# Other start addresses for six small tiles: 128 bytes more in each, taken from the dynamic transfers' scratch

## The chip, the cores and the metric

The kernel runs on one core of one Trainium2 chip. The metric is the device time in microseconds of one execution; the median of three runs before the change is 1042.14 us (1041.03 to 1042.35).

## The reference

One layer of a bidirectional encoder on 512 tokens of width 1024, in float32:

```
x += 1/2 * g1 * SwiGLU_1(mod(RMSNorm(x)))                                  # FFN 1
x += g2 * W_out( sig(gA) * W_A(WindowGQA+sink) + sig(gB) * W_B(DiffAttn) ) # the mixers
x += 1/2 * g3 * SwiGLU_2(mod(RMSNorm(x)))                                  # FFN 2
```

Shift, scale and gate of each step (`sh, sc, g`, nine vectors of 1024) come from a conditioning vector `c` through `w_mod`. `WindowGQA` is attention in a band of 128 positions (8 query heads, 2 key heads of 64); `DiffAttn` is dense attention of 4 heads, in which one softmax is taken from another, `p0 - lam * p1`. The gates `gA`, `gB` are 2 x 1024 columns of the mixers' input projection.

## The kernel before, in words

Everything lies transposed: 128 channels on the partitions, the 512 tokens along the free dimension. A float32 product is done as three products of type float32r: each operand is split into a high part and a low part (`split_from`, L188: ACT copies the high part, DVE subtracts, both counted under L189), and `mm3` (L172, its three matmuls are L173 to L175) adds high by high, high by low and low by high in PSUM. In the FFNs, `two` (L440, matmuls L446 to L448) does the same on halves of 256 tokens, in a Strassen-Winograd scheme (`Unit`) whose sums of weights are made by transfers that add into SBUF from the GpSimd queue (POOL). The matmuls of the mixers' first projections are L1168 to L1170 (512 columns) and L1187 to L1189 (`project_pairs`, 256 columns). The first operand of a matmul is called stationary here (128 columns of 4 bytes, loaded by its own instruction, PEld), the second moving (256 or 512 columns of 4 bytes).

The order of the work is fixed when the program is built: in some stages by hand (`manual_schedule`), in the mixers by a planner (`Line`) with fixed costs and due times, in which start addresses play no part.

All tiles lie in one SBUF pool. Every kind of tile has a tag and a fixed number of buffers; the buffers of a tag lie one behind another, and the tags in the order in which they are first asked for. Byte 0 on belongs to the scratch of dynamic transfers (4096 bytes a partition); the last tile ended at 229344 of 229376 bytes. In the built program the tiles that matter here began at these addresses in a partition:

| tile | what it holds | start, mod 128 | mod 256 |
|---|---|---|---|
| `high`, `low` | split weights, 5 slots of 4096 bytes each | 64; 0 with `ASIDE` (64 bytes on); 32 with `TURN` (96 bytes on) | 64; 128; 160 |
| `b8` | 12 tiles of 8192 bytes: hidden values, keys, values, activations | 64 | 64 |
| `raw`, `f2` | loaded weights; temporaries | 64 | 192 |
| `u4` | 6 tiles of 4096 bytes, see below | 32 | 160 |

`u4` (L157) serves many ends: columns of `w_mod` while a gate vector is made (`mod_load`, L240); operands of the FFNs' sums (`h_sum`, L589, the tile `n1`; `act_begin`, L1762, its last two spaces), where it is the moving operand of L446 to L448; weights that a transfer adds to (`Unit.place`, L469); small tables; and three uses that the change touches:

- **First gates' weights.** `load_split(..., spare=True)` (L210) puts the split weights of the first three gates into six `u4` tiles. `first_gates` (L1123) uses them as the stationary operand of `mm3`, in the hand-ordered stage between FFN 1 and the mixers (`boundary`, L360): 3 gates x 8 steps x 3 matmuls x 2 halves of 256 tokens = 144 matmuls. Between them stand small matmuls of the normalisation, L331 (`sums`) and L320 (`spread`).
- **Turned probabilities of the dense attention.** `diff_turn` (L1362) transposes the probabilities and splits them into two `u4` tiles; `diff_out` (L1379) takes 256 columns of them as the moving operand against `vb_h`, `vb_l` (in `b8`): 4 heads x 2 x 4 x 3 = 96 matmuls.
- **Turned probabilities of the window attention.** `window_turn` (L1598) and `window_out` (L1616) do the same with one `u4` tile per turn: 20 turns x 2 key heads x 3 = 120 matmuls against `vz` (in `b8`).

Of the kernel before, what the change touches and what calls it, by code (L numbers as in the profile page):

```python
# [12 lines left out]
F32R = mybir.dt.float32r  # L13
# [5 lines left out]
P = 128  # L19
D = 1024  # L20
T = 512
NC = D // P
# [111 lines left out]
def layer(ctx: ExitStack, tc: tile.TileContext, a: dict):  # L134
    nc = tc.nc
# [5 lines left out]
    def name(tag):  # L141
        count[0] += 1
        return f"{tag}_{count[0]}"

    def sbuf(tag, shape, dt, bufs):
        return sb.tile(shape, dt, name=name(tag), tag=tag, bufs=bufs)
# [7 lines left out]
    def b8(dt=F32R):  # L154
        return sbuf("b8", [P, 4, T], dt, 12)

    def u4(dt=F32R):  # L157
        return sbuf("u4", [P, 2, T], dt, 6)

    def small(n):  # L160
        return sbuf("sm", [P, 8], F32, 24)[:, 0:n]
# [4 lines left out]
    def keep(shape, nm, dt=F32):  # L166
        return sb.tile(shape, dt, name=nm, tag=nm, bufs=1)
# [20 lines left out]
    def split_from(hi, lo, src):  # L188
        last = S.copy(hi, src), V.tensor_tensor(lo, src, f(hi), ALU.subtract)  # L189
        split[:] = [i.ins for i in last]  # L190
# [5 lines left out]
    def high_low(n=1024, aside=0, holder=None):  # L196
        while turn[0] % HILO in holders:
            turn[0] += 1
        i = turn[0] % HILO
        turn[0] += 1  # L200
        if holder:
            holders[i] = holder
        i = i * 1024 + min(i, 2) * GAP + aside
        return tuple(t[:, i : i + n] for t in parts)
# [5 lines left out]
    def load_split(src, n=1024, spare=False, aside=0):  # L210
        raw = sbuf("raw", [P, 1024], F32, RAW)
        if spare:
            hi, lo = (u4().rearrange("p a b -> p (a b)") for _ in range(2))
        else:
            hi, lo = high_low(aside=aside)
        nc.sync.dma_start(raw[:, 0:n], src)
        split_from(hi[:, 0:n], lo[:, 0:n], raw[:, 0:n])
        return hi, lo
# [16 lines left out]
    parts, modv = [], []  # L235
# [4 lines left out]
    def mod_load(v, c, w=None):  # L240
        if w is None:
            w = u4(F32).rearrange("p a b -> p (a b)")
        nc.sync.dma_start(w, a["w_mod"][v * NC + c])
        return w
# [109 lines left out]
    def new_h():  # L354
        t = [b8() for _ in range(4)]
        hh = [t[c // 4][:, c % 4, :] for c in range(NC)]
        hl = [t[2 + c // 4][:, c % 4, :] for c in range(NC)]
        return hh, hl
# [245 lines left out]

    cact = [sbuf("ka", [P, D], F32, 1)]
    hh, hl = new_h()
    modv += [keep([P, NC], f"mod{v}") for v in range(len(modv), 9)]
    nc.scalar.dma_start(ccol, a["c"])
    tc.keep_in_program_order(nc.scalar.dma_start(par, a["par"]))
    for c in range(NC):  # L610
# [2 lines left out]
    with tc.manual_schedule(engines=BOUND | {mybir.EngineType.SP, mybir.EngineType.Pool}):  # L613
# [23 lines left out]
        def first_loads(k):  # L637
            scale = mod_load(SC1, k)
            if k == 0:
                kept.append(keep([P, NT], "pos", I32))  # L640
            shift = mod_load(SH1, k) if k == 0 else None
            raw = sbuf("raw", [P, 1024], F32, RAW)
            nc.sync.dma_start(raw, a["w1s"][k])
            w1[k] = [scale, shift or mod_load(SH1, k), raw]
# [52 lines left out]
        for k in range(3):  # L697
            first_loads(k)
# [91 lines left out]
        for k in range(1, NC):  # L790
# [21 lines left out]
            for outs in groups:  # L812
                for w, h in ((wh, hh[k]), (wh, hl[k]), (wl, hh[k])):
                    first_products(k, outs, w, h, FULL[0], False, k == NC - 1 and w is wl)
        loaded1 = [load_split(a["w1i"][0, k]) for k in range(2)]

    rest = [(v, c) for v in (G1, SC2, SH2, G2, SC3, SH3, G3) for c in range(NC)]
# [140 lines left out]
    with tc.manual_schedule(engines={mybir.EngineType.SP, mybir.EngineType.Pool}):  # L958
# [4 lines left out]
        for q in range(4, 2 * PLAIN):  # L963

            w, sums_from = loaded1, split[1]
            if q < 5:
                with tc.issue_after(split[0]), tc.issue_after(split[1]):
                    loaded1 = [load_split(a["w1i"][1, k]) for k in range(2)]
            behind = split[1]
            out = pair_banks()  # L970
            for k in range(NC):
                wh, wl = w[k // 4]
                for i in range(2):
                    o = (k % 4) * 256 + i * P
                    mm3(out[i], wh[:, o : o + P], wl[:, o : o + P], hh[k], hl[k], k == 0, k == NC - 1)
            with tc.issue_after(sums_from):
                for t in ("n1",) if q == 4 else ("n2", "t3", "t4"):
                    h_sum(t)
            with tc.issue_after(behind):
                finish(q, out)  # L980
            if q == 4:
                units1[PLAIN].prepare("s1")
            side1(1.0)
# [131 lines left out]
    def gate_end(j, out):  # L1115
        t = f2()
        S.activation(t, out, AF.Tanh, scale=0.5)
        S.dma_start(gate_scr[j], t)

    gate_w = [load_split(a["w_gate"][j], spare=True) for j in range(3)]  # L1120
    gate_out = {}

# [119 lines left out]
    def turned(srcs, tag="tp"):  # L1242

        tp = bank(tag)
        for j, src in enumerate(srcs):
            PE.transpose(tp[:, j * P : (j + 1) * P], src, ident)
        line.now += len(srcs) * TR
        line.free[tag] = line.helped(0.6, 0.8)
        return tp[:, 0 : len(srcs) * P]

    def cut(src, n):
        return [src[:, j * P : (j + 1) * P] for j in range(n)]
# [109 lines left out]
    def diff_turn(h, b, p):  # L1362

        tp = turned(cut(p, NT))
        turns["b"] += 1
        g, i = h * NT // 2 + b // 2, b % 2
        if i == 0:
            pair = [u4().rearrange("p a b -> p (a b)") for _ in range(2)]
            pt_b[g] = [t.rearrange("p (k i q) -> p k i q", k=NT, i=2) for t in pair]
        hi, lo = pt_b[g]  # L1370
        with tc.high_priority():
            split_from(hi[:, :, i, :], lo[:, :, i, :], tp.rearrange("p (k q) -> p k q", k=NT))
        if i == 1:
            line.at(
                line.free["tp"] + SLACK, lambda: diff_out(h, g),
                ("op" if g % 2 == 0 else "", lambda: turns["o"] == g + h),
            )

    def diff_out(h, g):  # L1379
        if g % 2 == 0:  # L1380
            out_b[h] = bank("op")
        hi, lo = pt_b[g]
        he = slice(h * P, (h + 1) * P)
        o = out_b[h][:, (g % 2) * 2 * P : (g % 2 + 1) * 2 * P]
        for k in range(NT):
            kh, kl = (t[:, k, :, :].rearrange("p i q -> p (i q)") for t in (hi, lo))
            mm3(o, vb_h[:, k, he], vb_l[:, k, he], kh, kl, k == 0, k == NT - 1)
        line.now += 2 * MM3
        turns["o"] += 1
        if g % 2:  # L1390
            t = f2()
            with tc.high_priority():
                S.copy(t, out_b[h])
            line.free["op"] = line.now + 1.0
            line.at(line.free["op"] + SLACK, lambda: diff_norm(h, t), ("op",))
# [137 lines left out]
    def span(b):  # L1533
        first, last = max(b - 1, 0), min(b + 1, NT - 1)
        return first, last - first + 1
# [59 lines left out]
    def turn_tag(b, g, kc):  # L1595
        return "acc" if (g + kc) % 2 else "tp"

    def window_turn(b, g, kc, sc):  # L1598
        tag = turn_tag(b, g, kc)
        tp = turned([sc[q][:, kc * P : (kc + 1) * P] for q in (0, 2, 1, 3)], tag)  # L1600
        pt = u4()
        with tc.high_priority():
            split_from(pt[:, 0, :], pt[:, 1, :], tp)
        i = g * span(b)[1] + kc
        line.at(
            line.free[tag] + SLACK, lambda: window_out(b, g, kc, pt),
            ("op" if i == 0 else "", lambda: turns["w"] == (b, i)),
        )
        if kc + 1 == span(b)[1]:
            turns["a"] += 1  # L1610
        else:
            line.at(line.now, lambda: window_turn(b, g, kc + 1, sc), (turn_tag(b, g, kc + 1),))
# [3 lines left out]
    def window_out(b, g, kc, pt):  # L1616
        first, nk = span(b)
        if g == 0 and kc == 0:
            out_a[b] = bank("op")
        o_ps = out_a[b]  # L1620
        for kv in range(2):
            vh, vl = (v[:, first + kc, kv, :, :].rearrange("p w d -> p (w d)") for v in wa["v"])
            ph, pl = (pt[:, i, kv * 2 * P : (kv + 1) * 2 * P] for i in range(2))
            mm3(
                o_ps[:, g * 2 * P : (g + 1) * 2 * P], vh, vl, ph, pl,
                kv == 0 and kc == 0, kv == 1 and kc == nk - 1,
            )
        line.now += MM3
        if g == 1 and kc == nk - 1:
            bq = slice(b * P, (b + 1) * P)  # L1630
            oa_h, oa_l = wa["o"]
            with tc.high_priority():
                split_from(oa_h[:, :, bq], oa_l[:, :, bq], o_ps.rearrange("p (g q) -> p g q", g=4))
            line.free["op"] = line.helped(0.6, 0.8)
            done["a"] += 1
            turns["w"] = (b + 1, 0)
        else:
            turns["w"] = (b, g * nk + kc + 1)
# [244 lines left out]
    with tc.manual_schedule(engines=BOUND):  # L1883
# [6 lines left out]
        at = TO_FFN2  # L1890
# [187 lines left out]
```

## Time and profile before

| what | value |
|---|---|
| median of three runs | 1042.14 us (1041.03 to 1042.35) |
| time of the profiled execution | 1040.55 us |
| its span, first to last instruction | 1038.8 us |
| PE, DVE, ACT, POOL busy | 1031.9, 786.8, 577.5, 167.7 us |
| DMA | 220.92 MB, 213 GB/s on average |

The span covers 1038.8 of the profiled execution's 1040.55 us, so 1.8 us lie around it. That execution is 0.5 us under the lowest of the three runs. Busy times of PE overlap, since one matmul's record (0.28 us for 256 columns) reaches over the start of the next two. So the cost of one more matmul is read from the timeline, as the distance between the starts of matmuls that follow each other; it is called the pitch here.

### The profile page before, as it was taken

The page shows a single profiled execution, that of the slowest core. Times are in us where ns is not written, and L with a number is a line of the kernel's source. Part 1 is how long each engine was busy: PE and PEld are TensorE (multiplying, and loading weights), DVE is VectorE, ACT ScalarE, POOL GpSimd, SP SyncE. Part 2 cuts the span into 40 slices and gives each one's busy share as a digit, 9 for nine tenths or more (in the row PEclk, how much of TensorE's full clock was granted, in tenths as well). Part 3 has the DMA queues.
Part 4 walks back from the last instruction along what each step waited for, and adds up shares of the span by engine and source line. Part 5 has one row for each costly group of instructions (what it writes and reads, how often), then busy time and mean ns, then how long its engine had stood idle before and what let it go on. Part 6 is the DMA issues. An engine that isn't in the chain of part 4 may idle for free.

```text
span 1038.8 us, 18730 instructions
## 1 busy us (share of the span) xinstructions
PE 1031.9 (99%) x7342; PEld 951.0 (92%) x7342; DVE 786.8 (76%) x1436; ACT 577.5 (56%) x952; POOL 167.7 (16%) x191
## 2 busy tenths in 40 slices
PE   9999999999999999999999999999999999999998
PEld 6889899899998998899888888989999999999998
DVE  7896667567797679859772588976899777877867
ACT  6665335244455333667785855525867546655553
POOL 2101110111100100543323101001112112212210
PEclk9999999999999999999999999999999999999999
DMA  9977887967884369796637934974498998989974
GB/s 366 357 231 203 237 235 219 254 153 225 233 202 156 129 219 409 236 263 150 173 79 183 270 123 157 377 231 100 97 237 193 237 235 207 227 223 214 204 153 112
DMA packets 68793, 220.92 MB, mean 213 GB/s; under 512 B 8288, under 2 KB 10976, under 8 KB 68704
## 3 DMA queue, kind: packets, MB, share of 16 engines
q1 hardware_dynamic: 46224, 146.52, 38.5%
q0 software_dynamic: 19344, 68.70, 35.9%
q10 hardware_dynamic: 3136, 4.51, 1.2%
q8 instruction: 57, 0.93, 0.4%
q14 instruction: 32, 0.26, 0.1%
HBM read 209.46 MB, written 10.23 MB: 211 GB/s over the span
## 4 chain that ended last, share of the span: by engine, by line
PE 94%; ACT 3%; DVE 3%; issue 0%; POOL 0%; DVEq 0%; ACTq 0%; POOLq 0%
PE acc L446 7%; PE acc L447 7%; PE acc L448 7%; PE sc L447 6%; PE sc L448 6%; PE sc L446 6%; PE sc L173 5%; PE sc L174 5%; PE sc L175 5%; PE acc L173 4%; PE acc L175 4%; PE acc L174 4%; PE acc L1168 2%; PE acc L1170 2%; PE acc L1169 2%; PE acc L691 1%
## 5 line engine op out<-in xcount | busy, mean ns | idle before, releaser
L189 ACT CAST high<-raw 128x1024 fp32r<-128x1024 f32 (+2 forms) x160 | 155.9, 985 | 151.3 <-PE sc L174 44.0
L189 DVE TENSOR_TENSOR low<-raw,high 128x1024 fp32r<-128x1024 f32 (+2 forms) x160 | 181.3, 1141 | 42.0 <-ACT high L189 40.6
L446 PE MATMUL acc<-b,high 128*128 128x256 f32 x508 | 140.8, 277 | 0.0
L447 PE MATMUL acc<-b,high 128*128 128x256 f32 x508 | 140.6, 277 | 0.1
L448 PE MATMUL acc<-b,low 128*128 128x256 f32 x508 | 140.5, 277 | 0.0
L447 PE MATMUL sc<-b,high 128*128 128x256 f32 x500 | 138.2, 276 | 0.0
L446 PE MATMUL sc<-b,high 128*128 128x256 f32 x500 | 138.1, 276 | 0.0
L448 PE MATMUL sc<-b,low 128*128 128x256 f32 x500 | 138.1, 276 | 0.0
L189 ACT CAST high<-u 128x1024 fp32r<-128x1024 f32 (+1 forms) x73 | 75.4, 1036 | 50.9 <-PE sc L174 19.9
L189 DVE TENSOR_TENSOR low<-u,high 128x1024 fp32r<-128x1024 f32 (+1 forms) x73 | 87.6, 1201 | 20.8 <-ACT high L189 19.0
L173 PE MATMUL sc<-b,high 128*128 128x512 f32 (+1 forms) x272 | 97.5, 358 | 0.0
L174 PE MATMUL sc<-b,high 128*128 128x512 f32 (+1 forms) x272 | 97.2, 357 | 0.0
L175 PE MATMUL sc<-b,low 128*128 128x512 f32 (+1 forms) x272 | 97.1, 357 | 0.0
L447 PEld LDWEIGHTS acc<-b,high 128*128 128x128 f32 x508 | 95.5, 188 | 0.4 <-DVE b L1862 0.3
L446 PEld LDWEIGHTS acc<-b,high 128*128 128x128 f32 x508 | 95.4, 188 | 0.3 <-ACT f L523 0.2
L448 PEld LDWEIGHTS acc<-b,low 128*128 128x128 f32 x508 | 95.4, 188 | 0.0
L446 PEld LDWEIGHTS sc<-b,high 128*128 128x128 f32 x500 | 93.9, 188 | 0.0
L448 PEld LDWEIGHTS sc<-b,low 128*128 128x128 f32 x500 | 93.9, 188 | 0.0
L447 PEld LDWEIGHTS sc<-b,high 128*128 128x128 f32 x500 | 93.9, 188 | 0.0
L173 PE MATMUL acc<-b,high 128*128 128x512 f32 (+1 forms) x240 | 89.2, 371 | 0.2 <-DVE u L189 0.2
L175 PE MATMUL acc<-b,low 128*128 128x512 f32 (+1 forms) x240 | 86.8, 362 | 0.0
L174 PE MATMUL acc<-b,high 128*128 128x512 f32 (+1 forms) x240 | 86.6, 361 | 0.0
(398 smaller groups left out, 2714.1 us busy)
## 6 DMA issues: line engine op xcount, KB each, us to landing
u<-w_mod SPq DMA_DIRECT2D x40, 512.0 KB, 8.4
b<-w_mod SPq DMA_DIRECT2D x32, 512.0 KB, 5.5
raw<-w2i SPq DMA_DIRECT2D x31, 512.0 KB, 5.2
u<-w2i POOLq DMA_DIRECT2D x31, 512.0 KB, 6.7
raw<-w1u SPq DMA_DIRECT2D x24, 512.0 KB, 6.9
u<-w1u POOLq DMA_DIRECT2D x24, 512.0 KB, 7.3
raw<-w1o SPq DMA_DIRECT2D x24, 384.0 KB, 4.6
raw<-w_gate SPq DMA_DIRECT2D x16, 512.0 KB, 5.3
```

Source lines behind the costliest of these rows:

```text
L173: PE.matmul(out, wh, xh, start=first, stop=False)
L174: PE.matmul(out, wh, xl, start=False, stop=False)
L175: PE.matmul(out, wl, xh, start=False, stop=last)
L189: last = S.copy(hi, src), V.tensor_tensor(lo, src, f(hi), ALU.subtract)
L446: PE.matmul(out, wh[:, s], xh, start=first and j == 0, stop=False, skip_group_check=True)
L447: PE.matmul(out, wh[:, s], xl, start=False, stop=False, skip_group_check=True)
L448: PE.matmul(out, wl[:, s], xh, start=False, stop=last and j == 1, skip_group_check=True)
L691: PE.matmul(out1[i][:, r], w[:, i * P : (i + 1) * P], h[:, r], start=first and r.start == 0, stop=last and r.stop == T, skip_group_check=True,
L1168: PE.matmul(out[t][:, 0:n], hh[k][:, ht], wh[:, o : o + n], start=k == 0, stop=False)
L1169: PE.matmul(out[t][:, 0:n], hh[k][:, ht], wl[:, o : o + n], start=False, stop=False)
L1170: PE.matmul(out[t][:, 0:n], hl[k][:, ht], wh[:, o : o + n], start=False, stop=k == NC - 1)
```

## The change

Each `u4` tile grows from 4096 to 4224 bytes, and its users get a view that begins `at` elements of 4 bytes into it: 8 (32 bytes) unless they ask for another place; the first gates' weights and both kinds of turned probabilities ask for 0. The scratch of dynamic transfers shrinks from 4096 to 2048 bytes a partition. The small tile `mod8` (the last of the nine gate vectors) is set up after the `u4` tiles instead of ahead of them.

```diff
-    def u4(dt=F32R):
-        return sbuf("u4", [P, 2, T], dt, 6)
+    def u4(dt=F32R, at=8):
+        return sbuf("u4", [P, 2 * T + 32], dt, 6)[:, at : at + 2 * T].rearrange("p (a b) -> p a b", a=2)
...
         if spare:
-            hi, lo = (u4().rearrange("p a b -> p (a b)") for _ in range(2))
+            hi, lo = (u4(at=0).rearrange("p a b -> p (a b)") for _ in range(2))
...
-    modv += [keep([P, NC], f"mod{v}") for v in range(len(modv), 9)]
+    modv += [keep([P, NC], f"mod{v}") for v in range(len(modv), 8)]
...
             if k == 0:
+                modv.append(keep([P, NC], "mod8"))
                 kept.append(keep([P, NT], "pos", I32))
...
-            pair = [u4().rearrange("p a b -> p (a b)") for _ in range(2)]
+            pair = [u4(at=0).rearrange("p a b -> p (a b)") for _ in range(2)]
...
-        pt = u4()
+        pt = u4(at=0)
...
-    nc = bacc.Bacc("TRN2", target_bir_lowering=False, num_devices=1, dynamic_dma_scratch_size=4096)
+    nc = bacc.Bacc("TRN2", target_bir_lowering=False, num_devices=1, dynamic_dma_scratch_size=2048)
```

No instruction is added, dropped or moved: on each of the five engines the built program holds the same instructions in the same order as before, apart from line numbers, running numbers in names and addresses. The same user gets the same one of the six `u4` buffers. What differs is where tiles lie:

- The six `u4` buffers begin at 165504 + 4224 i: 0 mod 128, and by turns 128 and 0 mod 256. A view at 8 begins at 32 mod 128, as before, by turns at 160 (as before) and at 32 mod 256. A view at 0 begins at 0 mod 128.
- Of the 144 matmuls of the first gates, 64 now have a stationary operand that starts from 128 mod 256, and 80 one from 0. Of the 216 with turned probabilities, 92 have a moving operand from 128 and 124 one from 0 mod 256. Of the 480 matmuls in the FFNs whose moving operand lies in `u4` (mod 128 unchanged), 264 start from 32 instead of 160 mod 256.
- All tiles ahead of `u4` move down by 2048 bytes, `raw`, `f2` and the tiles behind them by 1280 bytes. Both are multiples of 256, so nothing else changes mod 256.

## Prediction

> **What bounds the kernel now.** I read the page first: busy times, granted clock and the chain of work that ended last; then PE's own waits.
>
> ```profile
> span 1038.8 us, 18730 instructions
> ...
> PE 1031.9 (99%) x7342; PEld 951.0 (92%) x7342; DVE 786.8 (76%) x1436; ACT 577.5 (56%) x952; POOL 167.7 (16%) x191
> ...
> PEclk9999999999999999999999999999999999999999
> ...
> PE 94%; ACT 3%; DVE 3%; issue 0%; POOL 0%; DVEq 0%; ACTq 0%; POOLq 0%
> ```
>
> ```profile
> PE acc L620 <- POOL ident masks.py:199: 1.4, 1, 1.4
> PE acc L691 <- ACT b L678: 0.3, 1, 0.3
> PE acc L173 <- DVE u L189: 0.2, 1, 0.2
> PE acc L691 <- DVE b L685: 0.2, 1, 0.2
> ```
>
> The chain that sets the end is 94% PE, at a full granted clock, and PE's waits add up to 2.1 us. So the kernel takes as long as its matmuls stand apart, and a change that moves no instruction can act only through the pitch of matmuls, or by making somebody wait who did not wait before.
>
> **What a start address does to the pitch.** The change moves starts inside 128 bytes for two kinds of operand. The groups of PE, kept apart by shape, show that the tile matters although the shape is the same:
>
> ```profile
> L174 PE MATMUL acc<-b,u 128*128 128x256 f32 x48 | 13.5, 281 | 0.0
> ...
> L174 PE MATMUL op<-u,b 128*128 128x256 f32 x72 | 20.2, 281 | 0.0
> ...
> L447 PE MATMUL acc<-u,high 128*128 128x256 f32 x80 | 22.3, 279 | 0.0
> ...
> L447 PE MATMUL acc<-b,high 128*128 128x256 f32 x508 | 140.6, 277 | 0.1
> ...
> L447 PE MATMUL sc<-b,high 128*128 128x256 f32 x500 | 138.2, 276 | 0.0
> ```
>
> A matmul of 256 columns takes 276 to 277 ns with `b` and `high` (moving 64, stationary 0 mod 128), 279 with a moving `u` (32), 281 where the gates' weights (stationary 32) or turned probabilities (moving 32, stationary 64) take part. The pitch is read from the timeline, where each matmul has its row and three rows make a product.
>
> **Term 1, the first gates (144 matmuls).** The timeline of PE, first and last of 98 matmuls of the second half, nothing between them but their like:
>
> ```profile
> 363.75 0.28 PE L174 MATMUL acc<-b,u 128*128 128x256 f32 x1
> ...
> 375.26 0.28 PE L175 MATMUL acc<-b,u 128*128 128x256 f32 x1
> ```
>
> 11.51 us over 97 steps: 118.7 ns, with the stationary operand at 32. The same line in the same stage, just ahead of them, has it at 0 (`high` with `ASIDE`); first and last of 31 matmuls at 353 us, then of 36 at 343 us:
>
> ```profile
> 353.04 0.28 PE L175 MATMUL sc<-b,low 128*128 128x256 f32 x1
> ...
> 356.44 0.28 PE L175 MATMUL sc<-b,low 128*128 128x256 f32 x1
> ```
>
> ```profile
> 342.60 0.28 PE L173 MATMUL sc<-b,high 128*128 128x256 f32 x1
> ...
> 346.72 0.28 PE L175 MATMUL sc<-b,low 128*128 128x256 f32 x1
> ```
>
> 3.40/30 = 113.3 ns and 4.12/35 = 117.7 ns: with a start of 0 the stretch holds one of two rates until something interrupts it. The gates follow the fast stretch, so their first 18 matmuls should keep 113.3; small matmuls (L331, L320) cut the rest into stretches of 9, 9 and 108, and which rate the 108 fall into I can't tell. Ends: 144 x (118.7 - 113.3) = 0.78 us and 144 x (118.7 - 117.7) = 0.14 us. I take the fast rate for 36 (0.19) and the middle, 115.5, for 108 (0.35): **0.54 us gained**. Nothing takes it back here: DVE has written the weights of the stage behind before PE wants them.
>
> ```profile
> 370.37 4.63 DVE L189 TENSOR_TENSOR low<-raw,high 128x1024 fp32r<-128x1024 f32 x4 [0.45 <-ACT high L189]
> ```
>
> ```profile
> 375.38 0.40 PE L1168 MATMUL sc<-high,b 128*128 128x512 f32 x1
> ```
>
> All four low parts are there at 375.0 us, the first of them 1.2 us after 370.4; PE begins with the first at 375.4. So PE can come 3 us earlier before it waits here; without that lead the 0.54 us would be lost to DVE.
>
> **Term 2, turned probabilities (96 + 120 = 216 matmuls).** One burst of 12 in the dense attention, and 26 matmuls of `project_pairs`, which have a moving operand at 0 and a stationary one at 64, as the 216 will:
>
> ```profile
> 492.59 0.28 PE L173 MATMUL op<-u,b 128*128 128x256 f32 x1
> ...
> 493.91 0.28 PE L175 MATMUL op<-u,b 128*128 128x256 f32 x1
> ```
>
> ```profile
> 472.50 0.28 PE L1188 MATMUL acc<-low,b 128*128 128x256 f32 x1
> ...
> 475.44 0.28 PE L1189 MATMUL acc<-high,b 128*128 128x256 f32 x1
> ```
>
> 1.32/11 = 120.0 ns against 2.94/25 = 117.6 ns: 216 x 2.4 = **0.52 us gained**. Ends: nothing, and 216 x (120.0 - 113.3) = 1.45 us if they reach the fast rate. PE fills the time between bursts with gate products, so a shorter burst is a shorter kernel.
>
> The Trainium skill speaks against both terms: its page "TensorE: Matmul & The Clock Gate" (Step-by-step: what each phase is for) says that PE reads the moving operand and the next weights through two independent ports, so that loading weights takes nothing from the running matmul. By that sentence alone no start address would matter and the sum would be 0. The rows above differ by 6% between starts, and they decide.
>
> **What costs nothing.** The splits that write these tiles: a start of 32 (`u`) and of 64 (`b`) cost DVE the same, 686 and 688 ns, and DVE is busy 76%.
>
> ```profile
> L189 DVE TENSOR_TENSOR u<-tp,u 128x512 fp32r<-128x512 f32 x26 | 17.8, 686 | 13.1 <-ACT u L189 13.1
> ...
> L189 DVE TENSOR_TENSOR b<-tp,b 128x512 fp32r<-128x512 f32 x12 | 8.3, 688 | 14.8 <-ACT b L189 14.7
> ```
>
> The later `mod8` and the common shift of the other tiles change no distance mod 256. Of the 480 FFN matmuls with a moving `u4` operand, 264 start from 32 instead of 160 mod 256; the trace of before has no such case. I take 0; by the rows around it (a run of `u`, pitch 116.5 below) the ends are 264 x (116.5 - 113.3) = 0.84 us gained and 264 x (120.0 - 116.5) = 0.92 us lost.
>
> **Sum.** 0.54 + 0.52 = 1.06 us: the span goes from 1038.8 to 1037.7 us, the profiled execution from 1040.55 to 1039.5 us, and the median, which stands 1.6 us above that execution, from 1042.14 to **1041.1 us**, 0.1% less.
>
> **Rivals.**
>
> *Starts do not matter* (by the skill's two ports): the two rates belong to what runs before, not to the address, and the change does nothing: 1042.1 us. For it: the two rates at one address. Against it: the groups with a start of 32 take 279 to 281 ns on average, and those of 276 to 277 all have the moving operand at 64 and the stationary one at 0.
>
> *Slower: the FFNs lose their fast rate.* A stretch that comes from 512 columns runs slow; the run of `u` behind it (24 matmuls, 32 mod 128) ends in the fast rate, which the next 144 keep. First and last of 24, of 24 and of 139 matmuls:
>
> ```profile
> 141.29 0.28 PE L446 MATMUL acc<-b,high 128*128 128x256 f32 x1
> ...
> 144.00 0.28 PE L448 MATMUL acc<-b,low 128*128 128x256 f32 x1
> 144.12 0.28 PE L446 MATMUL sc<-u,high 128*128 128x256 f32 x1
> ...
> 146.80 0.28 PE L448 MATMUL sc<-u,low 128*128 128x256 f32 x1
> ...
> 147.50 0.28 PE L448 MATMUL acc<-b,low 128*128 128x256 f32 x1
> ...
> 163.14 0.28 PE L448 MATMUL sc<-b,low 128*128 128x256 f32 x1
> ```
>
> 2.71/23 = 117.8, 2.68/23 = 116.5 and 15.64/138 = 113.3 ns. If a run at 32 instead of 160 mod 256 no longer brings the fast rate, each later matmul costs 4.5 ns. L447 has 508 + 500 of them in the groups above, and L446 and L448 run beside it as often: for half of 3024 that is 6.8 us, and with the forecast's gain 1047.9 us. For it: in this place the rate hangs on what ran before, and the change moves half of it. Against it: 32 mod 128 stays, and so does the order. It decides from (2.08 + 1.06)/0.0045 = 700 matmuls, five such stretches.
>
> *Faster: the 512-column products between the bursts gain too.* They take longer in `acc`, between transposes and bursts, than undisturbed in `sc`:
>
> ```profile
> L175 PE MATMUL sc<-b,low 128*128 128x512 f32 x192 | 74.7, 389 | 0.0
> ...
> L175 PE MATMUL acc<-b,low 128*128 128x512 f32 x176 | 69.0, 392 | 0.0
> ```
>
> If a burst at 0 leaves them undisturbed, 528 x 3 ns = 1.6 us come on top: 1039.5 us.
>
> *The smaller scratch stalls POOL.* A transfer that adds would wait for room.
>
> ```profile
> q0 software_dynamic: 19344, 68.70, 35.9%
> ```
>
> ```profile
> u<-w2i POOLq DMA_DIRECT2D x31, 512.0 KB, 6.7
> ```
>
> A transfer of 512 KB to 128 partitions is 128 rows of 4 KB. 19344 packets are then at most 151 transfers, and at 6.7 us each there is 151 x 6.7/1038.8 = 0.97 in flight at a time on average, which speaks against it. For it: they come in groups. One that came a whole landing late would cost PE up to 6.7 us: 1047.8 us; it decides from half a landing, 3.2 us. The skill's page "DMA: Bandwidth & Descriptors" (SWDGE vs HWDGE vs iDMA) says that GpSimd's transfers keep descriptors of 16 bytes in rings in such a carveout; an estimate from it is 128 instead of 256 per ring. No row shows the room left.
>
> **How the numbers follow.** The forecast's case 0.64, starts that do not matter 0.14, the faster rival 0.11, lost fast rate 0.07, stalled POOL 0.04. About 0.2% (2.1 us) is what a measurement of this kernel can tell from no change. Faster by more: the faster rival and 0.02 of the forecast's upper tail, 0.13. Slower: the lost rate and 0.03 of the stalls, 0.10. Within: 0.77. The range takes in the bounds of the terms: 0.78 + 1.45 + 0.84 = 3.1 us below 1042.14, rounded to 1039.2, and 0.92 - 0.14 = 0.8 us above it, 1042.9; what is left out is most of the two slower rivals and the far end of the faster one, under 0.2.
>
> **What would show it.** In the trace of after: the matmuls of the gates' last 98 stand 113 to 118 ns apart and their group falls under 281 ns; bursts of turned probabilities stand 117.6 apart (group 279 to 280); the runs behind `u` in the FFNs keep 113.3 and their groups 276 to 277; PE's waits stay near 2 us. I am wrong if the gates or the bursts keep their pitch, if an FFN stretch is found at 118, or if PE gets a wait on a tile that POOL loads.

## The result, and the profile after

The change makes the kernel slower: the median is 1049.02 us (1048.61 to 1050.7, six runs) against 1041.64 us (1041.03 to 1042.35, six runs) of the kernel before, a ratio of 1.0069 with a 95% interval of 1.0058 to 1.008. The prediction was 1041.1 us, and the measured time lies outside its range. The profiled execution of after takes 1049.30 us, its span 1047.5 us. In the medians of the kernels below, three far slower runs (1136.01, 1606.52 and 3673.27 us) are left out, and with the second of them the trace of its kernel, `u4` at 192.

The page of after, busy times and the chain that ended last:

```profile
span 1047.5 us, 18730 instructions
...
PE 1040.1 (99%) x7342; PEld 959.1 (92%) x7342; DVE 787.6 (75%) x1436; ACT 577.0 (55%) x952; POOL 167.8 (16%) x191
...
PEclk9999999999999999999999999999999999999999
...
PE 92%; ACT 4%; DVE 4%; issue 1%; POOL 0%; DVEq 0%; ACTq 0%; POOLq 0%
```

The picture is that of before: PE 99% busy, the clock full, the chain PE. The view of PE's waits of after, the four longest:

```profile
PE acc L620 <- POOL ident masks.py:199: 1.4, 1, 1.4
PE tp L729 <- POOL sm L725: 0.5, 1, 0.5
PE acc L692 <- ACT b L679: 0.3, 1, 0.3
PE acc L173 <- DVE u L189: 0.3, 1, 0.3
```

The four rows add up to 2.5 us where those of before gave 2.1. So waits are 0.4 us of the 8.7 us by which the span grew; for nearly all the rest the same 7,342 matmuls stand further apart. Which ones, the groups say (line, tiles, shape, count, then busy us and mean ns of one); the page of after:

```profile
L446 PE MATMUL acc<-b,high 128*128 128x256 f32 x508 | 142.5, 280 | 0.0
L447 PE MATMUL acc<-b,high 128*128 128x256 f32 x508 | 142.3, 280 | 0.1
L448 PE MATMUL acc<-b,low 128*128 128x256 f32 x508 | 142.1, 280 | 0.0
L447 PE MATMUL sc<-b,high 128*128 128x256 f32 x500 | 139.1, 278 | 0.0
```

and the groups of after with shapes kept apart:

```profile
L447 PE MATMUL acc<-u,high 128*128 128x256 f32 x80 | 22.3, 279 | 0.0
...
L174 PE MATMUL op<-u,b 128*128 128x256 f32 x72 | 20.1, 280 | 0.0
...
L174 PE MATMUL acc<-b,u 128*128 128x256 f32 x48 | 13.4, 280 | 0.0
```

The groups that the change was expected to leave alone, `b` with `high` in the FFNs, rise from 277 and 276 to 280 and 278 ns. The FFN matmuls with a moving `u` (80 in this row), among which are those whose own start moved, keep 279. The gates (`acc<-b,u`) and the probabilities (`op<-u,b`) fall from 281 to 280, as they should. So the loss is not in the matmuls that moved but in those behind them.

The timeline of PE in after shows how. First and last matmul of four pieces that follow each other in FFN 1: a stretch of 144 with `b`; the first 12 of a run with `u`, from 32 mod 256; its last 12, from 160; and the stretch of 120 with `b` behind it:

```profile
148.45 0.28 PE L446 MATMUL acc<-b,high 128*128 128x256 f32 x1
...
164.68 0.28 PE L448 MATMUL sc<-b,low 128*128 128x256 f32 x1
164.79 0.28 PE L446 MATMUL acc<-u,high 128*128 128x256 f32 x1
...
166.08 0.28 PE L448 MATMUL acc<-u,low 128*128 128x256 f32 x1
166.20 0.28 PE L446 MATMUL acc<-u,high 128*128 128x256 f32 x1
...
167.49 0.28 PE L448 MATMUL acc<-u,low 128*128 128x256 f32 x1
167.60 0.28 PE L446 MATMUL sc<-b,high 128*128 128x256 f32 x1
...
181.62 0.28 PE L448 MATMUL op<-b,low 128*128 128x256 f32 x1
```

The first stretch stands at (164.68 - 148.45)/143 = 113.5 ns, the two halves of the run at 117.3 (1.29/11 each), and the last stretch at 14.02/119 = 117.8 ns. The same last stretch in the trace of before:

```profile
166.05 0.28 PE L446 MATMUL sc<-b,high 128*128 128x256 f32 x1
...
179.56 0.28 PE L448 MATMUL op<-b,low 128*128 128x256 f32 x1
```

13.51/119 = 113.5 ns. In the FFNs 24 such stretches stand behind a run with `u`, 3,348 matmuls in all. Counting a matmul as wide when the median of the nine pitches around it is 116 ns or more, and as narrow otherwise, before has some 20 wide ones and no stretch that is mostly wide; after has some 1,880 wide ones, and 11 stretches of the 24. 1,880 x 4.4 ns = 8.3 us.

Which 11 it is follows a rule. Of the 24 runs with `u`, 16 are 24 matmuls long (the others are 6 or 30). One comes from other work; of the 15 that come from a stretch with `b`, 14 turn the pitch over: 8 find it narrow and leave it wide, 6 find it wide and leave it narrow. The fifteenth, at 746 us, whose own matmuls stand at 118 to 119 ns, finds it narrow and leaves it so. Two stretches that follow each other in FFN 2 of after, each behind such a run, first and last matmul:

```profile
759.55 0.28 PE L446 MATMUL sc<-b,high 128*128 128x256 f32 x1
...
776.40 0.28 PE L448 MATMUL acc<-b,low 128*128 128x256 f32 x1
```

```profile
779.34 0.28 PE L446 MATMUL acc<-b,high 128*128 128x256 f32 x1
...
795.56 0.28 PE L448 MATMUL sc<-b,low 128*128 128x256 f32 x1
```

16.85/143 = 117.8 ns and 16.22/143 = 113.4 ns. In the trace of before every one of these runs left the pitch narrow, whichever it found.

Summed row by row over the timelines, each matmul up to the start of the next and pauses left out, the FFN matmuls with `b` (48 with the tile `ka` counted among them) take 2.0 us more in FFN 1 and 6.2 us more in FFN 2, those with `u` 0.2 us more, the gates 0.24 us less and the probabilities 0.49 us less. That is 7.6 us, and the medians differ by 7.4. The profiled executions differ by 1.3 us more, which is as much as the first projection matmul comes later. It stands at 14.37 us in before:

```profile
14.37 0.39 PE L691 MATMUL acc<-b,high 128*128 128x256 f32 x1
```

and at 15.63 us in after:

```profile
15.63 0.39 PE L692 MATMUL acc<-b,high 128*128 128x256 f32 x1
```

In a kernel that has the median of before (the smaller scratch alone, below) it stands at 15.31, and in another of about that time (the mixture swapped) at 15.65. So this is the early head of one execution, and not the change.

### The profile page after: what moved, and what is told of

It reads as the page before. It is cut to its first block, busy times and chain, and to the rows that moved or that the text cites. A ratio compares the mean times of both kernels' runs of the same rounds, so it can differ in the third digit from the quotient of the medians.

```text
span 1047.5 us, 18730 instructions
## 1 busy us (share of the span) xinstructions
PE 1040.1 (99%) x7342; PEld 959.1 (92%) x7342; DVE 787.6 (75%) x1436; ACT 577.0 (55%) x952; POOL 167.8 (16%) x191
## 4 chain that ended last, share of the span: by engine, by line
PE 92%; ACT 4%; DVE 4%; issue 1%; POOL 0%; DVEq 0%; ACTq 0%; POOLq 0%
PE acc L447 7%; PE acc L446 7%; PE acc L448 7%; PE sc L447 6%; PE sc L446 6%; PE sc L448 6%; PE sc L173 5%; PE sc L174 5%; PE sc L175 5%; PE acc L173 4%; PE acc L175 4%; PE acc L174 4%; PE acc L1171 2%; PE acc L1170 2%; PE acc L1169 2%; PE acc L692 1%
## 5 line engine op out<-in xcount | busy, mean ns | idle before, releaser
L446 PE MATMUL acc<-b,high 128*128 128x256 f32 x508 | 142.5, 280 | 0.0
L447 PE MATMUL acc<-b,high 128*128 128x256 f32 x508 | 142.3, 280 | 0.1
L174 PE MATMUL sc<-b,high 128*128 128x512 f32 (+1 forms) x272 | 97.1, 357 | 0.0
L175 PE MATMUL sc<-b,low 128*128 128x512 f32 (+1 forms) x272 | 97.1, 357 | 0.0
L175 PE MATMUL acc<-b,low 128*128 128x512 f32 (+1 forms) x240 | 86.7, 361 | 0.0
L174 PE MATMUL acc<-b,high 128*128 128x512 f32 (+1 forms) x240 | 86.5, 361 | 0.0
```

The costliest lines, as they stand in the source:

```text
L174: PE.matmul(out, wh, xl, start=False, stop=False)
L175: PE.matmul(out, wl, xh, start=False, stop=last)
L446: PE.matmul(out, wh[:, s], xh, start=first and j == 0, stop=False, skip_group_check=True)
L447: PE.matmul(out, wh[:, s], xl, start=False, stop=False, skip_group_check=True)
```

## The experiments

**The theory** after the result (A in the expectations): a 256-column stretch with `b` and `high` runs at 113.4 or at 117.8 ns, and keeps what it begins with; the runs with `u` set that; and a run that goes from 32 to 160 mod 256 in its middle turns it over, so that about every second stretch is wide. The rivals: the smaller scratch or the common shift of the tiles (B in the expectations), and the views at 0 mod 128 (C).

All kernels of these experiments but one (the scratch alone) have `u4` tiles of 4352 bytes (128 bytes more than after the change), so that the six buffers begin alike, at 128 mod 256. Diffs are against the kernel after. Each ratio is to runs of before on the same chip. In the table a stretch counts as wide if most of it stands at 117.8 ns in that kernel's trace; "32+160" is a run of 12 matmuls from 32 and then 12 from 160.

| kernel | moving `u4` in the FFNs, mod 256 | median, us | ratio to before, 95% | wide, of 24 |
|---|---|---|---|---|
| before | 160 | 1041.64 | | 0 |
| after | 32+160 | 1049.02 | 1.0069 (1.0058 to 1.008) | 11 |
| all begin alike | 160 | 1040.76 | 0.9992 (0.9983 to 1.0001) | 0 |
| scratch alone | 160 | 1041.65 | 1.0001 (0.9993 to 1.001) | 0 |
| alike, all views at 8 | 160 | 1042.15 | 1.0005 (0.9996 to 1.0014) | 0 |
| all at 32 | 32 | 1041.22 | 0.9997 (0.9989 to 1.0006) | 1 |
| mixture alone | 32+160 | 1049.34 | 1.0077 (1.0064 to 1.009) | 11 |
| mixture swapped | 160+32 | 1041.06 | 1.0001 (0.9992 to 1.0009) | 0 |
| all at 64 | 64 | 1055.39 | 1.0136 (1.0121 to 1.0152) | 24 |
| all at 192 | 192 | 1054.25 | 1.012 (1.0105 to 1.0136) | not counted |
| all at 128 | 128 | 1042.13 | 1.0005 (0.9996 to 1.0014) | 1 |
| half at 64, last | 160+64 | 1039.74 | 0.9987 (0.9979 to 0.9996) | 1 |
| half at 64, first | 64+160 | 1040.83 | 0.9994 (0.9985 to 1.0003) | 1 |
| half at 64, and act_begin | 160+64 | 1040.56 | 0.9991 (0.9982 to 1.0) | 1 |

### All six tiles begin alike

```diff
-        return sbuf("u4", [P, 2 * T + 32], dt, 6)[:, at : at + 2 * T].rearrange("p (a b) -> p a b", a=2)
+        return sbuf("u4", [P, 2 * T + 64], dt, 6)[:, at : at + 2 * T].rearrange("p (a b) -> p a b", a=2)
```

> The u4 tiles grow by 256 bytes instead of 128, so all six begin at 128 mod 256: a view at 8 starts at 160 mod 256 as before the change, a view at 0 at 128. The smaller scratch and the later mod8 stay. Theory A (the runs of 24 matmuls with a moving u4 lose their effect on the FFN stretches behind them because half of each run starts at 32 mod 256): every FFN stretch behind such a run goes back to 113.4 ns from start to start, the time falls by some 8 us to 1040 to 1041.5, a ratio of 0.998 to 1.000 to the kernel before. Theory B (the scratch, or the common shift of the other tiles, took the time): 1049, a ratio of 1.007, with the stretches still at 117.8 ns. Theory C (the first gates' weights and probabilities at 0 mod 128 took it): also 1049.

1040.76 us, and the stretch behind the run stands as before; first and last in its trace:

```profile
166.38 0.28 PE L446 MATMUL sc<-b,high 128*128 128x256 f32 x1
...
179.88 0.28 PE L448 MATMUL op<-b,low 128*128 128x256 f32 x1
```

13.50/119 = 113.4 ns. Theory A holds: scratch, `mod8`, the shift and the views at 0 are all still there, and the loss is gone.

### The smaller scratch alone

The kernel before with one edit:

```diff
-    nc = bacc.Bacc("TRN2", target_bir_lowering=False, num_devices=1, dynamic_dma_scratch_size=4096)
+    nc = bacc.Bacc("TRN2", target_bir_lowering=False, num_devices=1, dynamic_dma_scratch_size=2048)
```

> The kernel before with the scratch of 2048 bytes alone: all tiles move down by 2048 bytes, nothing else. Theory A: no change, 1041.6, ratio 1.000 within 0.001. Theory B: 1048 to 1049, ratio 1.006 to 1.007. Theory C: no change.

1041.65 us, ratio 1.0001: the scratch and the shift of all tiles cost nothing. Rival B falls.

### All views at 8

The kernel of the first experiment, with `u4()` instead of `u4(at=0)` in its three places.

> As the run with 256 bytes more in each u4, but all users at 8, so every operand starts at the same address mod 256 as before the change. Theory A: the time of before, 1041.6, ratio 1.000; what it stands above the run with views at 0 is the worth of the first gates and the turned probabilities, some 0.7 us (0.24 + 0.49 as summed over their matmuls in the trace of the change). Theory B: 1049. Theory C: 1041.6, and the run with views at 0 stands 7 us above it.

1042.15 us, ratio 1.0005: the time of before. The first experiment, whose views at 0 are the only difference, lies 1.4 us lower by the medians, and 1.0 us by the rows of the traces: the gates take 16.62 instead of 17.16 us (the one pause of over 230 ns in either trace left out) and the probabilities 26.87 instead of 27.37. So the two terms of the prediction are there, and rival C falls.

### All at 32

```diff
-    def u4(dt=F32R, at=8):
-        return sbuf("u4", [P, 2 * T + 32], dt, 6)[:, at : at + 2 * T].rearrange("p (a b) -> p a b", a=2)
+    def u4(dt=F32R, at=40):
+        return sbuf("u4", [P, 2 * T + 64], dt, 6)[:, at : at + 2 * T].rearrange("p (a b) -> p a b", a=2)
```

> 256 bytes more in each u4, users at 40 instead of 8: every moving u4 operand of the FFNs starts at 32 mod 256, none at 160; the views at 0 start at 128 mod 256. Theory A in the form 'a start of 32 does not bring the fast rate': no run brings it, so all stretches that come from 512 columns stay at 117.8 ns: up to 3000 x 4.4 ns = 13 us above before, ratio up to 1.013. Theory A in the form 'it is the mixture of 32 and 160 inside one run that turns the rate over': runs of one kind bring the fast rate as before, 1040 to 1041.5, ratio 0.998 to 1.000. Theories B and C: 1049.

1041.22 us. A start of 32 mod 256 brings 113.4 ns as well as one of 160, but for one stretch of 24. That one, at 777 us, follows a stretch whose pitch went from 113.3 to 117.8 ns at a pause (0.18 us between the starts at 768.07 and 768.25 us), and the run at 32 between them left it wide. What costs is not the new address; it is the two addresses in one run.

### The mixture alone, and the mixture swapped

Both on the kernel of the first experiment. The mixture of the change:

```diff
-        h_op[t] = [u4() for _ in range(2)] if t == "n1" else b8()
+        h_op[t] = [u4(at=40), u4(at=8)] if t == "n1" else b8()
...
-        spaces[:] = [b8] * 6 + [lambda: sbuf("ka", [P, 2, T], F32R, 1), u4]
+        spaces[:] = [b8] * 6 + [lambda: sbuf("ka", [P, 2, T], F32R, 1), lambda: u4(at=40)]
```

> The run with 256 bytes more in each u4 (1040.8 us), but the first of the two n1 tiles and the tile of act_begin at 40 instead of 8: each run of 24 FFN matmuls begins with 12 from 32 mod 256 and ends with 12 from 160, as after the change, and nothing else starts where the change put it. Theory A, mixture form (12 at 32 and then 12 at 160 turn the pitch of what follows over, so that about every second stretch runs at 117.8 ns): some 1,870 matmuls x 4.4 ns = 8.2 us more, 1049.0, ratio 1.007; the same stretches as after the change are slow. Rival (it needs also the u4 tiles of 4224 bytes, or the views at 0 mod 256): 1040.8 as without the mixture, ratio 0.999.

1049.34 us, with the same 11 wide stretches as after, and as many wide matmuls. The stretch in its trace:

```profile
167.66 0.28 PE L446 MATMUL sc<-b,high 128*128 128x256 f32 x1
...
181.67 0.28 PE L448 MATMUL op<-b,low 128*128 128x256 f32 x1
```

14.01/119 = 117.7 ns. These two edits alone make the whole loss. Swapped:

```diff
-        h_op[t] = [u4() for _ in range(2)] if t == "n1" else b8()
+        h_op[t] = [u4(at=8), u4(at=40)] if t == "n1" else b8()
```

> As the mixture alone, in the other order: 12 from 160 mod 256, then 12 from 32. Mixture form 1 (any change by 128 bytes inside a run turns the rate over): every second stretch at 117.8 ns as with the other order, some 1048 to 1049, ratio 1.006 to 1.007. Mixture form 2 (only the step from 32 to 160 does it; what ends a run decides, and 32 ends it as well as 160): all stretches at 113.4, 1040.8, ratio 0.999.

1041.06 us:

```profile
167.36 0.28 PE L446 MATMUL sc<-b,high 128*128 128x256 f32 x1
...
180.87 0.28 PE L448 MATMUL op<-b,low 128*128 128x256 f32 x1
```

13.51/119 = 113.5 ns. The same two kinds of address in the other order cost nothing: form 2 in the expectation. (The tile of `act_begin` stays at 160 here and was at 32 in the mixture alone; but it is used in FFN 2 only, and the stretches of FFN 1 differ already.)

### All at 64, at 192 and at 128

The edit of "all at 32" with `at=48`, `at=16` and `at=0`.

> 256 bytes more in each u4 and users at 48: every moving u4 operand of the FFNs starts at 64 mod 256, just as the b8 operands around it, so that a run differs from its neighbours by nothing in its start. Theory A (a run at 32 or 160 brings the fast rate to a stretch that comes slowly from 512 columns, and one at 64 keeps what it finds): the runs and all behind them stay at 117.8 ns until something else interrupts; some 3,000 matmuls x 4.4 ns = 13 us more, less what the u4 matmuls save, 1052 to 1056, ratio 1.010 to 1.014. Rival (the end of a tile or any pause brings the fast rate, whatever the start): stretches stay at 113.4 and the 480 matmuls in the runs fall from 116.9 to 113.4: 1.7 us less than the run with views at 8: 1039.1, ratio 0.9975.

1055.39 us, all 24 stretches wide. One piece of its trace, from the first matmul of a run to the last of the stretch behind it:

```profile
165.93 0.28 PE L446 MATMUL acc<-u,high 128*128 128x256 f32 x1
...
182.78 0.28 PE L448 MATMUL op<-b,low 128*128 128x256 f32 x1
```

16.85/143 = 117.8 ns. Where a run starts as the `b8` operands around it do, it changes nothing: the pitch that a stretch has when it comes from the 512-column products stays. The one exception is the run at 748 us, the same that is apart in after (at 746 us there): it found 113.3 ns and left 117.8. So it is the runs at another start that bring 113.4 ns in the kernel before.

> 256 bytes more in each u4 and users at 16: the moving u4 operands of the FFNs start at 192 mod 256, as their neighbours in b8 (64) mod 128 but 128 bytes apart mod 256. Theory 'mod 128': only a start that differs mod 128 from the operands around it brings the fast rate, so it goes as with 64: about 1055.4, ratio 1.013 to 1.014, all FFN stretches that come from 512 columns at 117.8 ns. Theory 'mod 256': what turned the rate over after the change was the step of 128 bytes, and a run at 192 makes two of them: at least some stretches at 113.4 ns, 1040 to 1049, ratio 0.999 to 1.007.

1054.25 us, by its time alone: as at 64. So a start that differs by 128 only doesn't bring the narrow pitch. The expected ratio was 1.013 to 1.014; it is 1.012, and its interval takes in 1.013 but not 1.014.

> 256 bytes more in each u4 and users at 0: the moving u4 operands of the FFNs start at 128 mod 256, that is 0 mod 128. Theory 'any start that differs mod 128 from the operands around it brings the fast rate': as with 32 or 160, 1040.8, ratio 0.999 to 1.000. Rival 'it takes a start of 32 mod 128': as with 64, 1055.4, ratio 1.013 to 1.014.

1042.13 us, which can't be told from before: 0 mod 128 brings the narrow pitch too. The runs themselves are slower, 119.0 ns on average for their 480 matmuls instead of 117.1, 0.9 us in all; the gates and the probabilities give about as much back.

### Half of each run at 64

On the kernel of the first experiment: 64 last, 64 first, and 64 last with the tile of `act_begin` there as well.

```diff
-        h_op[t] = [u4() for _ in range(2)] if t == "n1" else b8()
+        h_op[t] = [u4(at=8), u4(at=48)] if t == "n1" else b8()
```

> The run with 256 bytes more in each u4 (1040.8 us), but the second n1 tile at 48: a run of 24 has 12 from 160 mod 256 and then 12 from 64, as the b8 operands behind it. Theory A (the first 12 bring the fast rate, the last 12 keep it and run at 113.4 instead of 116.9): 240 x 3.5 ns = 0.8 us less, 1040.0, ratio 0.998. Rival (12 are not enough, or the step from 160 to 64 inside a run turns the rate over as the step from 32 to 160 does): half or all of the stretches at 117.8: 1046 to 1055, ratio 1.005 to 1.013.

1039.74 us, ratio 0.9987 (0.9979 to 0.9996): the one kernel of this study whose interval lies below 1. The run's second half and the stretch in its trace:

```profile
164.60 0.28 PE L446 MATMUL acc<-u,high 128*128 128x256 f32 x1
...
179.46 0.28 PE L448 MATMUL op<-b,low 128*128 128x256 f32 x1
```

14.86/131 = 113.4 ns: twelve matmuls from 160 are enough, and those from 64 keep the pitch. By the rows the `u` runs take 0.45 us less than before, where 0.8 was expected.

> The two n1 tiles of the run with half of each run at 64 exchanged: 12 from 64 mod 256 first, then 12 from 160. Theory A (the operands that differ mod 128 from those around them bring the fast rate wherever in the run they stand, those at 64 keep what they find): all stretches behind the runs at 113.4 ns, also the 72 matmuls at 746 us that stayed at 117.8 when 64 came last (0.3 us); the three runs that come slowly from 512 columns have their first 12 at 117.8 (0.15 us lost): 1039.6, ratio 0.998 to 0.999. Rival (the step from 64 to 160 in mid-run turns the rate over as the step from 32 to 160 does): about every second stretch at 117.8, 1047 to 1048, ratio 1.005 to 1.007.

1040.83 us. Neither order turns the pitch over here, as theory A said; but the 72 matmuls at 746 us stayed at 117.8, which it had wrong.

> The run with the second n1 tile at 64 mod 256 (1039.7 us), and the tile of act_begin there too (runs of 6 and 18 matmuls in FFN 2 that come fast from a run at 160). Theory A (64 keeps the rate that it finds, here the fast one): some 60 matmuls x 3.5 ns = 0.2 us less, 1039.5, ratio 0.998 to 0.999. Rival (a pause ahead of these runs takes the fast rate away and the start at 160 gave it back): stretches behind them at 117.8 ns, up to 330 matmuls x 4.4 ns = 1.5 us more, 1041.2, ratio 1.000.

1040.56 us, not 1039.5. By the rows the FFNs' runs save another 0.2 us, as expected, but the gates' last 108 matmuls stand near 118 in this trace and take 0.44 us more, at the addresses that gave 113.7 with 64 last (rows below, under term 1). These three and the first experiment lie within 1.1 us and can't be ranked by their intervals.

## Why the prediction was wrong, point by point

**What bounds the kernel.** Right: the matmuls' pitch moved the time; PE's waits grew by 0.4 us.

**Term 1, the gates.** The sign was right; 0.54 us was forecast, 0.24 measured, between the ends of 0.14 and 0.78. The first 18 stood at 113.4 as said. The 108 were put in the middle, at 115.5, and fell into the wide pitch; second and last of them in after:

```profile
365.95 0.28 PE L174 MATMUL acc<-b,u 128*128 128x256 f32 x1
...
378.44 0.28 PE L175 MATMUL acc<-b,u 128*128 128x256 f32 x1
```

12.49/106 = 117.8 ns. With all tiles alike (the first experiment), 99 of them:

```profile
364.23 0.28 PE L173 MATMUL acc<-b,u 128*128 128x256 f32 x1
...
375.34 0.28 PE L175 MATMUL acc<-b,u 128*128 128x256 f32 x1
```

11.11/98 = 113.4 ns. The starts don't decide this by themselves. The kernels with 64 last, and with 64 last and `act_begin`, differ only in a tile that FFN 2 uses, long after the gates. Second and last of the 108 in the first of them and in the second:

```profile
362.41 0.29 PE L174 MATMUL acc<-b,u 128*128 128x256 f32 x1
...
374.46 0.28 PE L175 MATMUL acc<-b,u 128*128 128x256 f32 x1
```

```profile
363.40 0.28 PE L174 MATMUL acc<-b,u 128*128 128x256 f32 x1
...
375.89 0.28 PE L175 MATMUL acc<-b,u 128*128 128x256 f32 x1
```

12.05/106 = 113.7 ns and 12.49/106 = 117.8 ns, with the same matmuls from the same starts up to here. So this pitch can differ from one execution to another (these two were on different chips), and the term's size in one trace hangs on it; nothing in this study says what decides it.

**Term 2, the probabilities.** Right: 0.52 forecast, 0.49 measured. A burst of 12 in after:

```profile
495.72 0.28 PE L173 MATMUL op<-u,b 128*128 128x256 f32 x1
...
497.00 0.28 PE L175 MATMUL op<-u,b 128*128 128x256 f32 x1
```

1.28/11 = 116.4 ns, where the one of before quoted in the prediction stood at 120.0; inside all bursts the mean went from 119.6 to 117.3.

**What costs nothing: the step that failed.** The prediction took 0 for the 264 FFN matmuls that start from 32 instead of 160 mod 256, with ends of 0.84 us gained and 0.92 lost. For those matmuls that was right: they cost 0.2 us. But the ends priced only the matmuls that move, although the prediction's own rows showed that the stretch behind a run takes its pitch from it. The unknown had to be carried to the 3,348 matmuls behind: 4.4 ns each, up to 14.7 us. The case stood there as a rival, "the FFNs lose their fast rate", with 1047.9 us for half of them; some 1,880 came wide, 56%. That this number came so near is luck: the rival let a run at 32 no longer bring the narrow pitch, and took half because the change moves about half of the runs' matmuls, while in the runs 32 by itself does bring it, and the half comes from the turning over. The rival was given 0.07 because 32 mod 128 and the order stay. The kernel with all at 32 shows that this reason was sound for either address by itself, but for one stretch. What it overlooked stood in the change's own description: buffers of 4224 bytes begin by turns at 128 and 0 mod 256, and `n1` takes two of them, so one run holds both. The mixture alone reproduces the loss: 1049.34 us, the same 11 stretches.

**The other free items.** Right: the scratch and the shift cost nothing (ratio 1.0001), the splits showed no new wait on PE, and PE waited for no transfer of POOL. The faster rival didn't come either: the groups of 512 columns in `acc` keep 391 and 392 ns (L174, L175). And starts do matter: the same instructions in the same order took 1039.74 to 1055.39 us.

**The range.** It took in the ends of the moved matmuls only; with the rival's end it would have reached past 1049.

Left open: why the step from 32 to 160 mod 256 turns the pitch over and the step from 160 to 32 doesn't, what a pause does to the pitch, and what sets the gates' pitch. What was shown is which orders of addresses do it, not the cause inside PE.

## What to carry to other kernels

A tile size that isn't a multiple of the distance on which a start acts (here 256 bytes) gives its buffers different starts; before resizing, list the start of every operand for each buffer, in the order in which PE meets them. If a stretch of matmuls keeps the pitch it begins with, price an unknown at a few matmuls by all that stand behind them until the next reset. A tuned time can rest on an accident: here the narrow pitch of some 3,300 matmuls hung on a scratch tile that starts 32 bytes off its neighbours mod 128, and the kernel with all at 64 pays 14 us for lining it up.

## What the runs showed of the hardware

- Matmuls of 256 columns with a moving start of 64 and a stationary start of 0 mod 128, back to back, have two pitches, 113.4 and 117.8 ns (records of 276 and 281 ns), and hold either over 72 to over 300 matmuls, at a granted clock of 0.999 to 1.0. The Trainium skill, "TensorE: Matmul & The Clock Gate" (Step-by-step: what each phase is for), has two independent ports for the moving operand and the weights, and by that nothing to tell the two apart; these traces show two pitches 4% apart at one shape, one clock and the same addresses.
- A run at 0 or 32 mod 128 inside such a stretch left it at 113.4 ns almost always (in the seven traces with one kind of run, or with 160 ahead of 32, at most one of the 24 stretches is wide), a run at 64 mod 256 left it as it was in 22 of 23 cases, and 12 from 32 then 12 from 160 mod 256 turned it over in 14 of 15 cases, from 113.4 to 117.8 ns and back. The 24 matmuls behind the 512-column products at 141, 212 and 272 us stood at 117.8 in all of them.
- A pause of PE inside a stretch can change its pitch too. At 314 to 318 us two matmuls behind each other start 0.2 to 0.3 us apart; behind them the pitch stayed at 113.3 ns in before, went from 113.3 to 117.8 with all six tiles alike, and from 117.8 to 113.3 in after.
- The small matmuls at the start of the program moved the first projection by up to 1.3 us from one profiled execution to another (14.37 to 15.63 us), with kernels of about unchanged time at 15.31 and 15.65.
